# Two weight buffers for the modulation, eight tiles in the recurrence, and the channel DFT's fold computed early

## The chip, the cores and the metric

The kernel runs on one core of one Trainium2 chip. Its metric is the device time of one execution in microseconds (us). The time before is the median of three runs. The profile is of one further execution of its own.

## The reference, cut to what matters

The function is two layers of a diffusion backbone over 1024 latent tokens and 256 context tokens (1280 together), with a model width of 1024. Layer 0 is a bidirectional gated linear recurrence beside a Fourier mixer; layer 1 is latent attention. Each layer is modulated by a shift, a scale and a gate that come from a conditioning vector:

```python
def adaln(cond, w, b):
    return jnp.split(jax.nn.silu(cond) @ w + b, 3, axis=-1)      # w is 1024 x 3072, per layer

def rglru_coeffs(xc, gate_w, gate_b, lam):                       # per head of 64 channels, per direction
    r, i = sigmoid(gates of xc)
    log_a = -LRU_C * r * softplus(-lam)
    a = exp(log_a)
    b = sqrt(-expm1(2.0 * log_a)) * (i * xc)
    return a, b                                                  # then h[t] = a[t] * h[t-1] + b[t], both ways

def fourier_mix(u, w, b):
    ug = u.reshape(b_, length, FNET_GROUPS, FNET_GROUP_DIM)
    f = jnp.fft.fft2(ug, axes=(1, 3), norm='ortho').real
    return jnp.einsum('blgi,gij->blgj', f, w).reshape(b_, length, FNET_WIDTH) + b
```

In `fourier_mix` the transform over the 128 channels of a group and the 128 x 128 matrix `w` of that group are both linear maps of the channels, so the kernel folds them into one pair of tables: cos times `w` and sin times `w`.

## The kernel before

The kernel keeps the 1280 tokens in the free dimension and 128 channels in the partitions. Matrices of float32 are split into a high and a low part, and a product is three matmuls (high by high, high by low, low by high).

**Start (L145 to L308).** `ada_part` multiplies the condition with layer 0's shift and scale weights in four parts, from 32 loads of 256 KB through eight buffers (L209). `u0` (L238) loads one of eight tiles of the input through three buffers of the pool `xt`, modulates it and splits it into `uh` and `ul`. The word list `ORD` (L39) sets the order of these loads. The matmuls of the first two input projections, `in0(12)` and `in0(0)`, run as soon as their `uh` and `ul` are there.

**Recurrence (L445 to L521).** An input projection `in0(m)` (L262) is 24 groups of three matmuls (512, 512 and 256 tokens) into a PSUM tile `z`, of which there are two (L137). For each j from 0 to 6 the kernel runs `in0(j + 1)` and `in0(13 + j)`, that is 48 groups or slots, and hangs all other work of the recurrence on these slots through `slots0(j)` (L470). I call one such round of 48 slots a round. Among that work are six pieces of `gates` (L362), the convolution, the chain of tanh, exp, square, root and the two scans on ScalarE, VectorE and GpSimd (L383), the splits of the next weights (`w0_high` on VectorE, `w0_low` on GpSimd) and `ada_next` (L461).

**The modulation's other weights.** Layer 1's shift and scale (`adam`, L173) and both layers' gates (`adag`) are 16 units in `ada_work` (L252): each loads 1 MB (L174), multiplies it by the condition in eight matmuls (L165) into a tile of the PSUM pool `g_ps`, which has two tiles (L138) and also serves the gates, and adds the result to a row on VectorE (L183). Two further entries without a load finish a row. A round calls `ada_next` at slots 0, 38 and 44 while units are left, which is in rounds 0 to 5. The pool `adaw` (L312) has one buffer of 1 MB, so the load for a unit can start only when the matmuls of the unit before it are done, and `ada_next` issues it right behind them.

**Order.** Inside `manual_schedule` (L459) the order on TensorE, VectorE, ScalarE and GpSimd is the one that `slots0` writes down. The order of the loads on SyncE (SP) is left to the framework's scheduler, which issues a load when it takes its buffer to be free; on the chip SP then waits, in order, for each load's buffer.

**Tiles of the recurrence.** `lt` (L359) hands out tiles of 128 x 1280 from a ring of nine: per round r and i of both directions, th and aa of both directions, eight in all.

**Fourier mixer (L534 on).** The pool `ft` is opened when the recurrence's pools are closed, so its tiles lie where tiles of the recurrence were, and a load or a write into it waits for the last use of what lay there. The folded tables `cw` and `sw` (L134) are computed here: `fw`, `cosd` and `sind` are loaded from ScalarE's queue (L541 to L544), and in `fourier(0)` (L561) two float32 matmuls of 512 columns, `dft_c` and `dft_s`, write two `g_ps` tiles which ScalarE copies to `cw` and `sw`. Before them in TensorE's order stands `in0(9)`; behind them stand the first transform matmuls `aps` (L605), which read `cw`, and `in0(10)`, which needs the PSUM tile that `in0(8)` has filled and that ScalarE's copy `fu` (L567) empties.

Of the kernel before, what the change touches and what calls it, by code (L numbers as in the profile page):

```python
# [13 lines left out]
F32 = mybir.dt.float32  # L14
# [7 lines left out]
P = 128  # L22
# [31 lines left out]
def _body(ctx, tc, ap, out, dbg=None):  # L54
# [42 lines left out]
    o = 0  # L97
# [31 lines left out]
    V.tensor_scalar(out=vneg, in0=vpos, scalar1=-8.0, scalar2=None, op0=ALU.mult)  # L129
    V.tensor_scalar(out=vpos, in0=vpos, scalar1=8.0, scalar2=None, op0=ALU.mult)  # L130
    sp_c()


    cw = const.tile([P, 512], F32, name="cw")  # L134
    sw = const.tile([P, 512], F32, name="sw")
# [173 lines left out]
            u0(i)  # L309
    xt_c()  # L310
    a0_c()
    aw_p, aw_c = pool("adaw", 1, side="right")  # L312

    lru = None

# [40 lines left out]
        else:  # L356
            V.tensor_tensor(out=hls[j][1], in0=xcs[j], in1=f(hls[j][0]), op=ALU.subtract)

    def lt(nm):  # L359
        return lru.tile([P, T], F32, tag="lt", bufs=9, name=nm)  # L360

    def gates(j, d, c):  # L362

        def run():
            a, n = CH3[c]
            if c == 0:
                for g in range(2):
                    gt[j, d, g] = lt(f"gate{d}{g}_{j}")
            gh, gl = gws[j]
            xh, xl = hls[j]  # L370
            ps = [gtile(f"gps{j}{d}{c}{h}") for h in range(2)]
            for i, (w, x) in enumerate(((gh, xh), (gh, xl), (gl, xh))):
                for h in range(2):
                    r = slice(64 * h, 64 * h + 64)
                    TE.matmul(ps[h][:, :n], w[r, d, :], x[r, a : a + n], start=(i == 0), stop=(i == 2))  # L375
            for h in range(2):
                for g in range(2):
                    r = slice(64 * g, 64 * g + 64)
                    S.activation(out=gt[j, d, g][64 * h : 64 * h + 64, a : a + n], in_=ps[h][r, :n], func=AF.Sigmoid,  # L379
                                 bias=vv("gateb", 4 * j + 2 * h + d)[r, :])  # L380
        return run

    def chain(j):  # L383

        c = {}

        def tanh(d):
            th[j, d] = lt(f"th{d}_{j}")
            S.activation(out=th[j, d], in_=gt[j, d, 0], func=AF.Tanh, scale=vpos[:, 8 * d + j : 8 * d + j + 1])

        def exp(d):
            aa[j, d] = lt(f"aa{d}_{j}")
            S.activation(out=aa[j, d], in_=gt[j, d, 0], func=AF.Exp, scale=vneg[:, 8 * d + j : 8 * d + j + 1])

        def square(d):
            S.activation(out=gt[j, d, 0], in_=aa[j, d], func=AF.Square)

        def beta(d):
            V.scalar_tensor_tensor(out=th[j, d], in0=gt[j, d, 0], scalar=1.0, in1=th[j, d], op0=ALU.add, op1=ALU.mult)  # L399

        def root(d):
            S.activation(out=th[j, d], in_=th[j, d], func=AF.Sqrt)

        def drive(d):
            G.tensor_tensor(out=gt[j, d, 1], in0=gt[j, d, 1], in1=xcs[j], op=ALU.mult)

        def scaled(d):
            V.tensor_tensor(out=gt[j, d, 1], in0=gt[j, d, 1], in1=th[j, d], op=ALU.mult)  # L408

        def scan(d):  # L410
            r, i, a = th[j, d], gt[j, d, 1], aa[j, d]
            if d == 0:
                c1, c2, e = slice(0, NC), slice(NC, T), slice(NC - 1, NC)
            else:
                c1, c2, e = slice(NC - 1, None, -1), slice(T - 1, NC - 1, -1), slice(0, 1)
            V.tensor_tensor_scan(out=r[:, c1], data0=a[:, c1], data1=i[:, c1], initial=0.0, op0=ALU.mult, op1=ALU.add)  # L416
            V.tensor_tensor_scan(out=r[:, c2], data0=a[:, c2], data1=i[:, c2], initial=r[:, e], op0=ALU.mult, op1=ALU.add)

        def both():
            G.tensor_tensor(out=th[j, 0], in0=th[j, 0], in1=th[j, 1], op=ALU.add)  # L420
            if "hs" in dbg:
                load(dbg["hs"][j], th[j, 0])

        def gated():
            sg = sgs_.pop(j)
            V.tensor_tensor(out=sg, in0=sg, in1=th[j, 0], op=ALU.mult)
            put(j, sg)

        for n, u in (("tanh", tanh), ("exp", exp), ("square", square), ("beta", beta), ("root", root),
                     ("drive", drive), ("scaled", scaled), ("scan", scan)):  # L430
            for d in range(2):
                c[n, d] = lambda u=u, d=d: u(d)
        c["both"], c["gated"] = both, gated
        return c
# [19 lines left out]
    x_split(0, 1)  # L454
    w0_load(1)
    w0_dma(13)
    ada_work[0][0]()
    order0 = ExitStack()
    order0.enter_context(tc.manual_schedule(engines={e.engine for e in (TE, V, S, G)}))  # L459

    def ada_next():  # L461
        if ada_work:
            _, u = ada_work.pop(0)
            u()
        if ada_work and ada_work[0][0]:
            ada_work[0][0]()

    ch = {}

# [67 lines left out]
    evs = ft_p.tile([P, 640], F32, name="ev")  # L537
    ods = ft_p.tile([P, 640], F32, name="od")
    fold = ft_p.tile([P, 4, 256], F32, name="fold")
    fw = ft_p.tile([P, 512], F32, name="fw")  # L540
    S.dma_start(out=fw, in_=ap["fw"])  # L541
    dft = [ft_p.tile([P, P], F32, name=n) for n in ("cosd", "sind")]
    for d, n in zip(dft, ("cosd", "sind")):
        S.dma_start(out=d, in_=ap[n])  # L544
    tabs = {}
    for n in ("cos_h", "cos_l", "sin_h", "sin_l"):
        t = ft_p.tile([P, 2, 2, 256], F32R, name=n)
# [10 lines left out]
    def fourier(g, work=()):  # L558

        z = in0(8 + g, work) if g else z8  # L560
        if g == 0:  # L561
            for d, o, n in zip(dft, (cw, sw), "cs"):
                ps = gtile(f"dft_{n}")
                TE.matmul(ps, d, fw, start=True, stop=True)
                S.copy(out=o, in_=ps)
        u, ev, od = fus[g % 2], evs, ods
        S.copy(out=u, in_=z[:, :T])  # L567
        cg, sgm = cw[:, P * g : P * g + P], sw[:, P * g : P * g + P]
# [939 lines left out]
```

## Time and profile before

| | us |
|---|---|
| median of three runs | 1500.9 |
| the three runs | 1502.68, 1500.90, 1496.44 |
| the profiled execution | 1506.19 |
| its span in the profile | 1504.4 |

| engine | busy us | share of the span |
|---|---|---|
| TensorE matmul (PE) | 1416.8 | 94% |
| VectorE (DVE) | 944.1 | 63% |
| GpSimd (POOL) | 684.0 | 45% |
| ScalarE (ACT) | 597.2 | 40% |

The span is the time from the first to the last instruction of the profiled execution; the 1.8 us around it are not in the profile. The shares are means over stages with different limits, so the start (to about 63 us), the recurrence (63 to 392 us) and the entry of the Fourier mixer (392 to 430 us) have to be read for themselves. In a timeline row the text in square brackets is the time for which the engine stood idle before the row, and what ended it.

### The profile page before, as it was taken

The numbers are of one execution on the slowest core, as the hardware profiler recorded it, in microseconds if no ns is written. First come the engines' busy times: TensorE is split into PE (matmuls) and PEld (weight loads), VectorE is DVE, ScalarE is ACT, GpSimd is POOL, SyncE is SP. The second block draws the span as 40 slices with busy tenths as digits, with TensorE's granted clock in tenths as the row PEclk, the third lists the DMA queues.
The fourth block names the chain that finished last, engine by engine and source line by source line (L and its number), as shares of the span: only waits on it lengthen the run. The fifth ranks groups of instructions, "written<-read, shape, count | busy, mean of one in ns | idle before, by whom it ended". The sixth has DMA issues, their size and how long they took to land.

```text
span 1504.4 us, 19960 instructions
## 1 busy us (share of the span) xinstructions
PE 1416.8 (94%) x7912; PEld 993.6 (66%) x7912; DVE 944.1 (63%) x1454; ACT 597.2 (40%) x756; POOL 684.0 (45%) x314
## 2 busy tenths in 40 slices
PE   6978998898789999999999999999999999999996
PEld 3756675576568878887987675555555555555685
DVE  4538787799456524233954537576665757574799
ACT  2268676688611222111432133433443334445210
POOL 1124243344311114330422128766856776699642
PEclk9999999999989999999999999999999999999998
DMA  8522223311130455322043121101201010124442
GB/s 299 209 88 103 90 105 116 123 60 46 46 93 29 146 195 180 112 90 68 5 126 116 64 84 32 50 15 53 74 19 36 29 36 15 36 64 140 133 129 82
DMA packets 65869, 133.05 MB, mean 88 GB/s; under 512 B 5864, under 2 KB 32744, under 8 KB 63472
## 3 DMA queue, kind: packets, MB, share of 16 engines
q1 hardware_dynamic: 63328, 123.79, 25.3%
q0 software_dynamic: 2016, 7.60, 1.4%
q8 instruction: 62, 1.02, 0.3%
q10 hardware_dynamic: 432, 0.39, 0.1%
q14 instruction: 31, 0.25, 0.1%
HBM read 100.09 MB, written 24.66 MB: 83 GB/s over the span
## 4 chain that ended last, share of the span: by engine, by line
PE 62%; DVE 17%; issue 5%; DMA 4%; POOL 2%; ACT 1%; SPq 0%; DVEq 0%; POOLq 0%; ACTq 0%
PE s L1197 12%; PE y L770 10%; PE po L1213 10%; PE mx L1100 6%; PE z L270 5%; PE in1g L84 2%; PE in1g L86 2%; PE in1g L85 2%; DVE xc L339 2%; DVE hf L1384 1%; DMA adawg<-in_ada_g 1%; DVE gate L408 1%; DVE th L416 1%; POOL th L420 1%; DVE th L399 1%
## 5 line engine op out<-in xcount | busy, mean ns | idle before, releaser
L1203 POOL TENSOR_TENSOR ra<-ra,p 128x1024 f32<-128x1024 f32 x112 | 268.5, 2397 | 97.1 <-ACT p L1199 94.4
L1102 DVE TENSOR_REDUCE m<-mx 128x1 f32<-128x512 f32 (+1 forms) x384 | 210.1, 589 | 101.5 <-PE mx L1100 100.9
L1199 ACT ACTIVATE p<-s 128x1024 f32<-128x1024 f32 x160 | 163.3, 1024 | 210.5 <-PE s L1197 207.7
L293 POOL TENSOR_TENSOR w0l<-w,w0h 128x1024 fp32r<-128x1024 f32 x24 | 69.2, 2883 | 280.5 <-DVE w0h L77 196.4
L270 PE MATMUL z<-uh,w0h 128*128 128x512 f32 (+1 forms) x576 | 154.7, 376 | 4.4 <-ACT uh L75 4.3
L270 PE MATMUL z<-ul,w0h 128*128 128x512 f32 (+1 forms) x576 | 151.2, 370 | 0.0
L270 PE MATMUL z<-uh,w0l 128*128 128x512 f32 (+1 forms) x576 | 147.8, 364 | 0.0
L379 ACT ACTIVATE gate<-gps,vec 64x512 f32<-64x512 f32 (+1 forms) x192 | 117.4, 612 | 47.1 <-PE gps L375 44.2
L270 PEld LDWEIGHTS z<-uh,w0h 128*128 128x128 f32 x576 | 97.9, 194 | 39.4 <-issue 18.4
L270 PEld LDWEIGHTS z<-ul,w0h 128*128 128x128 f32 x576 | 97.8, 193 | 27.5 <-issue 10.0
L270 PEld LDWEIGHTS z<-uh,w0l 128*128 128x128 f32 x576 | 96.5, 191 | 21.2 <-issue 4.1
L1197 PE MATMUL s<-R,KR 33*128 33x512 f32 (+1 forms) x640 | 101.8, 392 | 0.0
L1100 PE MATMUL mx<-Kh,Qh 64*128 64x512 f32 (+1 forms) x384 | 84.1, 404 | 3.9 <-DVE m L1102 3.9
L1100 PEld LDWEIGHTS mx<-Kh,Qh 64*128 64x128 f32 x384 | 39.5, 185 | 70.6 <-DVE m L1102 31.9
L1213 PE MATMUL po<-p,v_odd 128*64 128x512 f32 x320 | 79.2, 616 | 0.0
L1213 PE MATMUL po<-p,v_even 128*64 128x512 f32 x320 | 79.1, 616 | 0.0
L1100 PE MATMUL mx<-KR,R 64*128 64x512 f32 (+1 forms) x384 | 73.0, 356 | 0.0
L1197 PE MATMUL s<-Qh,Kh 64*128 64x512 f32 x320 | 70.3, 431 | 0.0
L1197 PEld LDWEIGHTS s<-R,KR 33*128 33x128 f32 (+1 forms) x640 | 61.6, 184 | 12.9
L773 DVE TENSOR_TENSOR n<-gbc,y 128x1024 f32<-128x1024 f32 x10 | 12.2, 1221 | 85.9 <-PE y L770 85.9
L1238 DVE RECIPROCAL ri<-ri 128x128 f32<-128x128 f32 x64 | 59.3, 937 | 9.9 <-ACT ri L1233 9.9
L1197 PE MATMUL s<-Ql,Kh 64*128 64x512 f32 x320 | 64.0, 391 | 0.0
(358 smaller groups left out, 3021.5 us busy)
## 6 DMA issues: line engine op xcount, KB each, us to landing
w<-in_w SPq DMA_DIRECT2D x24, 512.0 KB
adaw<-in_ada SPq DMA_DIRECT2D x32, 256.0 KB
adawm<-in_ada SPq DMA_DIRECT2D x8, 1024.0 KB
adawg<-in_ada_g SPq DMA_DIRECT2D x8, 1024.0 KB
y_dr<-sg SPq DMA_DIRECT2D x10, 640.0 KB
woraw<-in_wo SPq DMA_DIRECT2D x12, 512.0 KB
xt<-in_x_cm SPq DMA_DIRECT2D x8, 640.0 KB
yra<-y_dr SPq DMA_DIRECT2D x10, 512.0 KB
```

The source lines that it names most:

```text
L84: TE.matmul(o, lh, rh, start=start, stop=False)
L270: TE.matmul(z[:, a : a + n], wi[:, kt, :], ui[kt][:, a : a + n], start=(kt == 0 and ui is uh and wi is wh), stop=(kt == KT - 1 and wi is wl))
L293: G.tensor_tensor(out=wl, in0=wr.pop(m), in1=f(wh), op=ALU.subtract)
L379: S.activation(out=gt[j, d, g][64 * h : 64 * h + 64, a : a + n], in_=ps[h][r, :n], func=AF.Sigmoid, bias=vv("gateb", 4 * j + 2 * h + d)[r, :])
L770: TE.matmul(ps[:, 512 * hf : 512 * hf + 512], a[k], b[k][:, 512 * hf : 512 * hf + 512], start=(k == 0 and a is yh and b is woh), stop=(k = ...
L1100: TE.matmul(ps[a][:, :n], q[r, P * t : P * t + P], k[r, a0 : a0 + n], start=st, stop=not st)
L1102: V.tensor_reduce(out=m3s[t][:, a, i : i + 1], in_=ps[a][:, :n], axis=AX.X, op=ALU.max)
L1197: TE.matmul(ps[:, a, :], k[r, ks], w[r, c], start=(j == 0), stop=(j == len(parts) - 1))
L1199: S.activation(out=es, in_=ps, func=AF.Exp, scale=SCALE)
L1203: G.tensor_tensor(out=ra, in0=st["e"][0] if kt == 1 else ra, in1=es, op=ALU.add)
L1213: TE.matmul(st["o"][64 * a : 64 * a + 64, :], quad[q][6][:, k, 128 * i + 64 * a : 128 * i + 64 * a + 64], st["e"][k][:, a, :], start=(k == ...
L1238: V.reciprocal(out=st["ri"][:, d], in_=st["ri"][:, d])
```

## The change

- The pool `adaw` gets two buffers. Two of its loads are issued ahead of the recurrence, and `ada_next` then issues the load of the unit after the next one.
- `lt` no longer takes the next of nine tiles. Eight tiles have fixed names, and a table says for each round which tile of the round before each new tile takes over.
- `fw`, `cosd` and `sind` are loaded, and `cw` and `sw` computed, between the start's pools and the recurrence, in a pool `dq` that is closed at once. The loads are now on SP's queue. The same lines go from the Fourier mixer.

```diff
@@ -309,7 +308,19 @@
             u0(i)
     xt_c()
     a0_c()
-    aw_p, aw_c = pool("adaw", 1, side="right")
+    aw_p, aw_c = pool("adaw", 2, side="right")
+
+
+    dq_p, dq_c = pool("dq", side="right")
+    fw = dq_p.tile([P, 512], F32, name="fw")
+    load(fw, ap["fw"])
+    for o, n, nm in ((cw, "cosd", "c"), (sw, "sind", "s")):
+        d = dq_p.tile([P, P], F32, name=n)
+        load(d, ap[n])
+        ps = gtile(f"dft_{nm}")
+        TE.matmul(ps, d, fw, start=True, stop=True)
+        S.copy(out=o, in_=ps)
+    dq_c()
 
     lru = None
 
@@ -356,8 +367,15 @@
         else:
             V.tensor_tensor(out=hls[j][1], in0=xcs[j], in1=f(hls[j][0]), op=ALU.subtract)
 
-    def lt(nm):
-        return lru.tile([P, T], F32, tag="lt", bufs=9, name=nm)
+
+    LT = ["r0", "i0", "r1", "i1", "th0", "th1", "aa0", "aa1"]
+    lts = {-1: {n: i for i, n in enumerate(LT)}}
+
+    def lt(j, n):
+        if j not in lts:
+            o = lts[j - 1]
+            lts[j] = dict(zip(LT, (o[k] for k in ("r0", "r1", "i0", "aa0", "i1", "aa1", "th0", "th1"))))
+        return lru.tile([P, T], F32, tag=f"lt{lts[j][n]}", name=f"{n}_{j}")
 
     def gates(j, d, c):
 
@@ -365,7 +383,7 @@
             a, n = CH3[c]
             if c == 0:
                 for g in range(2):
-                    gt[j, d, g] = lt(f"gate{d}{g}_{j}")
+                    gt[j, d, g] = lt(j, f"{'ri'[g]}{d}")
             gh, gl = gws[j]
             xh, xl = hls[j]
             ps = [gtile(f"gps{j}{d}{c}{h}") for h in range(2)]
@@ -385,11 +403,11 @@
         c = {}
 
         def tanh(d):
-            th[j, d] = lt(f"th{d}_{j}")
+            th[j, d] = lt(j, f"th{d}")
             S.activation(out=th[j, d], in_=gt[j, d, 0], func=AF.Tanh, scale=vpos[:, 8 * d + j : 8 * d + j + 1])
 
         def exp(d):
-            aa[j, d] = lt(f"aa{d}_{j}")
+            aa[j, d] = lt(j, f"aa{d}")
             S.activation(out=aa[j, d], in_=gt[j, d, 0], func=AF.Exp, scale=vneg[:, 8 * d + j : 8 * d + j + 1])
 
         def square(d):
@@ -454,7 +472,8 @@
     x_split(0, 1)
     w0_load(1)
     w0_dma(13)
-    ada_work[0][0]()
+    for k in range(2):
+        ada_work[k][0]()
     order0 = ExitStack()
     order0.enter_context(tc.manual_schedule(engines={e.engine for e in (TE, V, S, G)}))
 
@@ -462,8 +481,8 @@
         if ada_work:
             _, u = ada_work.pop(0)
             u()
-        if ada_work and ada_work[0][0]:
-            ada_work[0][0]()
+            if len(ada_work) > 1 and ada_work[1][0]:
+                ada_work[1][0]()
 
     ch = {}
 
@@ -537,11 +556,6 @@
     evs = ft_p.tile([P, 640], F32, name="ev")
     ods = ft_p.tile([P, 640], F32, name="od")
     fold = ft_p.tile([P, 4, 256], F32, name="fold")
-    fw = ft_p.tile([P, 512], F32, name="fw")
-    S.dma_start(out=fw, in_=ap["fw"])
-    dft = [ft_p.tile([P, P], F32, name=n) for n in ("cosd", "sind")]
-    for d, n in zip(dft, ("cosd", "sind")):
-        S.dma_start(out=d, in_=ap[n])
     tabs = {}
     for n in ("cos_h", "cos_l", "sin_h", "sin_l"):
         t = ft_p.tile([P, 2, 2, 256], F32R, name=n)
@@ -558,11 +572,6 @@
     def fourier(g, work=()):
 
         z = in0(8 + g, work) if g else z8
-        if g == 0:
-            for d, o, n in zip(dft, (cw, sw), "cs"):
-                ps = gtile(f"dft_{n}")
-                TE.matmul(ps, d, fw, start=True, stop=True)
-                S.copy(out=o, in_=ps)
         u, ev, od = fus[g % 2], evs, ods
         S.copy(out=u, in_=z[:, :T])
         cg, sgm = cw[:, P * g : P * g + P], sw[:, P * g : P * g + P]
```

## Rows read from the trace of the kernel before

**Rows 1.** The page, part 2: busy tenths of TensorE in 40 slices of the span.

```profile
PE   6978998898789999999999999999999999999996
```

**Rows 2.** Waits of TensorE, 0 to 430 us: waiter, released by, us, times, longest.

```profile
PE adam L165 <- DMA adawm<-in_ada: 11.9, 4, 5.4
PE adag L165 <- DMA adawg<-in_ada_g: 11.8, 4, 4.4
PE dft_c L564 <- DMA cosd<-in_cosd: 11.8, 1, 11.8
```

**Rows 3.** Timeline of TensorE, units at slots 0, 38, 44: start, us, what, [idle].

```profile
63.10 1.07 PE L165 MATMUL adam<-adawm,cond 128*32 128x512 f32 x8
...
105.00 1.94 PE L165 MATMUL adam<-adawm,cond 128*32 128x512 f32 x8 [5.39 <-DMA adawm<-in_ada]
...
111.82 1.07 PE L165 MATMUL adam<-adawm,cond 128*32 128x512 f32 x8 [1.34 <-DMA adawm<-in_ada]
...
141.39 1.06 PE L165 MATMUL adam<-adawm,cond 128*32 128x512 f32 x8
...
150.80 1.94 PE L165 MATMUL adam<-adawm,cond 128*32 128x512 f32 x8 [4.64 <-DMA adawm<-in_ada]
...
157.75 1.06 PE L165 MATMUL adam<-adawm,cond 128*32 128x512 f32 x8 [0.55 <-DMA adawm<-in_ada]
...
237.84 1.93 PE L165 MATMUL adag<-adawg,cond 128*32 128x512 f32 x8 [4.44 <-DMA adawg<-in_ada_g]
...
244.85 1.07 PE L165 MATMUL adag<-adawg,cond 128*32 128x512 f32 x8 [1.41 <-DMA adawg<-in_ada_g]
...
283.31 1.93 PE L165 MATMUL adag<-adawg,cond 128*32 128x512 f32 x8 [4.12 <-DMA adawg<-in_ada_g]
...
290.28 1.07 PE L165 MATMUL adag<-adawg,cond 128*32 128x512 f32 x8 [1.85 <-DMA adawg<-in_ada_g]
```

**Rows 4.** Windows: PE, PEld, DVE, ACT, POOL busy (count), PEclk, DMA share, GB/s.

```profile
150.80:155.50 4.70, 4.70 (x16) 2.56 (x17) 0.69 (x1) 0.28 (x1) 0.00 (x0) 0.50 0.32 90
290.28:326.21 35.93, 35.93 (x194) 26.80 (x194) 32.90 (x22) 27.89 (x35) 15.98 (x5) 1.00 0.23 78
```

**Rows 5.** Timeline of SP's queue, loads issued, 47 to 145 us.

```profile
47.62 1.19 SPq L60 DMA_DIRECT2D w<-in_w  x2
...
143.84 0.33 SPq L60 DMA_DIRECT2D w<-in_w  x1
144.26 0.38 SPq L60 DMA_DIRECT2D adawm<-in_ada  x1
```

**Rows 6.** Timeline of VectorE and ScalarE in round 1, 147 to 150 us.

```profile
148.01 0.67 DVE L183 TENSOR_TENSOR adarow<-adarow,adam 128x512 f32<-128x512 f32 x1
...
147.37 2.41 ACT L396 ACTIVATE gate<-aa 128x1280 f32<-128x1280 f32 x2
```

**Rows 7.** The end of the start: VectorE's timeline, then two windows.

```profile
52.53 2.91 DVE L81 TENSOR_TENSOR ul<-xt,uh 128x1280 fp32r<-128x1280 f32 x2
...
54.00:58.00 4.00, 4.00 (x23) 3.38 (x22) 2.13 (x3) 0.17 (x1) 0.00 (x0) 1.00 0.70 281
58.00:62.00 4.00, 4.00 (x22) 3.42 (x21) 1.69 (x2) 1.07 (x1) 3.15 (x2) 1.00 0.13 30
```

**Rows 8.** Timeline of TensorE and ScalarE at the Fourier mixer's entry, 416 to 426 us.

```profile
416.18 2.04 PE L564 MATMUL dft_c<-fw,cosd 128*128 128x512 f32 x2 [11.76 <-DMA cosd<-in_cosd]
418.01 1.89 PE L564 MATMUL dft_s<-fw,sind 128*128 128x512 f32 x2
424.32 2.04 PE L605 MATMUL aps0a<-cw,fold 128*128 128x128 f32 x8 [4.42 <-DVE fold L582]
...
419.76 2.35 ACT L567 COPY fu<-z 128x1280 f32<-128x1280 f32 x2 [14.35 <-DVE sg L426]
```

**Rows 9.** Timeline of VectorE and ScalarE in round 2, scan and second direction's gates.

```profile
167.19 2.35 DVE L417 TENSOR_TENSOR_SCAN th<-aa,th,gate 128x1024 f32<-128x1024 f32 x1
...
176.55 2.80 ACT L379 ACTIVATE gate<-gps,vec 64x512 f32<-64x512 f32 x4 [0.97 <-PE gps L375]
```

## The prediction

> **What bounds the kernel now.** I read the page's slices first, then the waits of TensorE, and then the timelines at the places that those waits name. In the slices TensorE is busy nearly everywhere; the lower digits lie in the first third [rows 1]. So time is to be gained only where TensorE stands still there. The waits name three such places among the changed code: the `adam` units wait 11.9 us for their loads, the `adag` units 11.8 us, and `dft_c` 11.8 us for `cosd` [rows 2]. The rest is not touched by the change.
>
> The timeline shows which units wait. In rounds 0, 1, 3 and 4 the unit at slot 44 waits 5.39, 4.64, 4.44 and 4.12 us for a load that was issued only when the unit at slot 38 was done, and the unit at the next round's slot 0 waits again for 1.34, 0.55, 1.41 and 1.85 us [rows 3]. Behind the longer wait TensorE runs at the lower of its two clock levels, 1.2 GHz: the granted clock is 0.50 from 150.80 to 155.50 us [rows 4], and the eight matmuls of the unit take 1.94 us where they take 1.06 without a wait [rows 3]. Round 2 has its last entry without a load, and round 5 has units at slots 0 and 38 alone and then a bare addition, so neither has this pattern.
>
> **The change, part by part.**
>
> *Two buffers.* The load issued behind the slot-38 unit now feeds not the next unit but the one after it, at slot 0 of the next round. The slot-44 unit finds its data, since they were asked for behind the slot-0 unit some forty slots earlier. What is late next is the slot-0 unit. I leave its load where it is in SP's queue: in round 1 it stands behind a weight load that SP releases at 143.84 us, is issued at 144.26 [rows 5], and is there when the unit starts at 150.80 [rows 3]. So the new start of the slot-0 unit is the old start of the slot-44 unit, and each of the four rounds becomes shorter by the difference of two rows [rows 3]:
> 111.82 - 105.00 = 6.82; 157.75 - 150.80 = 6.95; 244.85 - 237.84 = 7.01; 290.28 - 283.31 = 6.97; together 27.75 us.
> This holds the clock's part too. It holds only if TensorE is ready by then. In round 1 it may start the slot-44 unit at 150.80 - 4.64 = 146.16, and that unit with its four groups took 157.75 - 0.55 - 150.80 = 6.40 us at the half clock, so about 3.2 at the full one: it is ready at 149.4 and waits 1.4 us. The same sum gives 2.2, 1.2 and 0.9 us in rounds 0, 3 and 4: nearly 6 us of waiting stay, where there were 23.7.
> Nor may another engine be later than the load. The unit needs a `g_ps` tile that VectorE's addition of the slot-38 unit frees, and that ends at 148.01 + 0.67 = 148.68; the squares that the next round's first step needs end at 147.37 + 2.41 = 149.78 [rows 6]. Both are before 150.80, by 2.1 and 1.0 us. Can VectorE keep the shorter round? Round 5, with two units and no long wait, took 35.93 us at a VectorE busy for 32.90 of them, with TensorE never idle [rows 4]; the four rounds come down from about 46 to 39 us, which is longer. The first two loads go out together at the end of the start; the unit that needs the first stands at 63.10 [rows 3], and the transfer engines are at 0.13 of their time from 58 to 62 us [rows 7], so 1 MB more there is taken as free; without that room the slot-0 unit of round 0 would wait some 3.6 us, 1 MB at 281 GB/s [rows 7].
> Bounds of this part: if nothing is left to wait for at slot 0, the rounds save 9.0 + 8.4 + 8.2 + 7.9 = 33.5 us; if each remaining wait drops the clock as the long one does (4.7 us at half speed, 2.35 lost), they save 27.75 - 9.4 = 18.4. Idle times of 1.34 to 1.85 us were followed by units of 1.07 us, at the full clock [rows 3]; so I take 27.75.
>
> *The channel DFT at the Fourier entry.* Here 11.76 us of waiting and 3.72 us of matmuls (416.18 to 419.90) go [rows 8], but the path does not run through them. ScalarE's copy `fu` starts at 419.76, behind VectorE's last product of the recurrence, and the first transform at 424.32, behind VectorE's fold of that copy [rows 8]. By the pools' sizes `fu` still lies over a tile which that product reads, so both stay. What opens is that `in0(10)` may start when the first of the two copies is done, about 420.9, and fill TensorE until 424.32. This is worth 3.4 us if the scheduler places it before the transforms, and 0 if not. I take 1.2, nearer to nothing, as work behind a long idle time starts at the half clock.
>
> *The channel DFT at the start.* The same two matmuls, 3.72 us behind an idle TensorE, take half, 1.86, at the full clock, and they now lie where TensorE is busy for 4.00 of 4.00 us at a granted 1.00 [rows 7]: +1.86, between 0 and 3.72. `fw` lies in `dq` over the third buffer of `xt` (counting the pools from the right end of SBUF), whose last reader is the split `ul`, done at 52.53 + 2.91 = 55.44 [rows 7]. If the scheduler puts `dft_c` into TensorE's order before `fw` is there, `in0` queues behind it, and VectorE and GpSimd with the next weights behind that. Ahead of `fw` SP has 3.4 MB to load from about 47.6 us on [rows 5] (two weight tiles, two units, gate weights and a bias); at 281 GB/s [rows 7] that is done at 59.7, and 0.4 MB more at 61.0. So the wait is 0 to 61.0 - 55.4 = 5.6 us; I take 1.3, nearer to 0, because a place in the order later by some groups hides it. ScalarE gets two copies where it is busy for 1.07 of 4.00 us [rows 7], and its queue loses three loads; both count nothing.
>
> *A rule weighed.* These loads leave a queue of their own for SP's. The Trainium skill, "DMA: Bandwidth & Descriptors", section "Queues, rings and completion order", says that an engine takes the descriptors of one ring in order and alternates between different queues. By that rule the constants would have shared the engines from ScalarE's queue, and on SP's they come after all 3.4 MB: the wait would be 5.6 and not 1.3, and the sum 4.3 us higher. No row here shows two queues loading at once.
>
> *Eight tiles.* The gates of the second direction now write tiles that the first scan of the round before read last. That scan ends at 167.19 + 2.35 = 169.54 and the gates write from 176.55 [rows 9], a margin of 7.0 us counted within one round, which the change leaves alone; the first direction's gates stand in ScalarE's order behind the root that already waits for the last reader of their tiles. So 0.
>
> **The sum.** -27.75 + 1.86 + 1.3 - 1.2 = -25.8 us. The span of 1504.4 becomes 1478.6, the execution of 1506.2 becomes 1480.4. The median of the three runs is 5.3 us below the profiled one, so I set the sum against it: 1500.9 - 25.8 = 1475.
>
> **The rivals.**
> 1. *No wait is left*: the slot-0 load comes before 149 us because the scheduler moves it ahead of the weight load. Then the rounds save 33.5 and the time is 1469. For it: only SP's order holds the load back. Against it: that order has no reason to change.
> 2. *The constants come late*, behind all that SP has to load, or the remaining waits drop the clock: 5.6 us for `fw` gives 1479.4, the clock's 9.4 on top 1489. For it: SP's 3.4 MB. Against it: idle times under 2 us kept the clock.
> 3. *The second buffer doesn't help*: SP issues the load behind the slot-44 unit after all, the rounds keep their length and only the sum's rest stays, +2.0: 1503, within the bound of no change. Against it: in round 1 SP issued the load 1.8 us after the slot-38 unit's end.
> 4. *Slower, by the eight tiles*: if the first scan ends later than 18.8 us after the round's start (11.8 now), ScalarE's gates wait for it, hold both `g_ps` tiles, and TensorE stops, in seven rounds. It outweighs 25.8 us from 3.7 us a round, that is with the scan 10.7 us later than now; at 12 us later it costs 35 and gives 1510. Against it: VectorE starts each round afresh, waiting for the slot-0 unit.
>
> **How the numbers follow.** Forecast (1470 to 1482) 0.62; rival 1 (1463 to 1470) 0.15; rival 2 (1482 to 1493) 0.14; rival 3 (1493 to 1508) 0.05; rival 4 0.04. A measurement of this kernel can tell about 0.5%, 7.5 us, from no change, so faster holds the first three: 0.91, the same 0.05, slower 0.04. The range has to take in rival 1 with the open 3.4 us (1464) and most of rival 2: 1463 to 1490.
>
> **What the changed profile would show.** Right: the slot-44 units without an idle time, the slot-0 units with 1 to 2 us of it, the wait for `adam` and `adag` loads near 6 us in all, rounds 0, 1, 3 and 4 near 39 us, the granted clock at 1.00 through them, `fu` still behind the last product. Wrong: a wait of ScalarE's gates for VectorE's scan, a `dft_c` that stands idle for more than some 3 us at the start, or slot-0 units that wait for 5 us, which would show the load still behind the unit.

## The result: 1477 us, and the profile after

The changed kernel takes 1477.0 us (median of four runs, 1476.0 to 1477.7); the kernel before, beside it on the same chip, 1501.6. The ratio is 0.9842, with a 95% interval from 0.9819 to 0.9866: 24.6 us faster by the medians, where 25.8 were forecast, and inside the range. Its profiled execution took 1476.0 us at a span of 1474.3.

The page's slices first: TensorE's busy tenths and the granted clock in 40 slices of the changed kernel's span. The sevens and eights that stood in the third to the ninth slice in [rows 1] are nines now; the eleventh, with the Fourier entry, fell from 7 to 5.

```profile
PE   6999999998599999998999999999999999999997
...
PEclk9999999999799999999999999999999999999999
```

Then TensorE's waits of the changed kernel, 0 to 430 us (waiter, released by, us, times, longest). Against [rows 2] the units' waits have come down from 23.7 us in eight waits to 5.2 in four, and `dft_c` is gone from the list. A wait of 17.3 us behind ScalarE's copy `fu` stands in its place at the Fourier entry.

```profile
PE z L269 <- ACT fu L576: 17.3, 1, 17.3
...
PE adam L164 <- DMA adawm<-in_ada: 3.1, 2, 2.1
...
PE adag L164 <- DMA adawg<-in_ada_g: 2.1, 2, 1.4
```

The timeline of TensorE in the changed kernel: the first unit, the units at slots 44 and 0 around the ends of rounds 0, 1, 3 and 4, and at 188.17 the first unit of round 3 (start, us, what, idle time before). These answer to [rows 3].

```profile
65.84 1.07 PE L164 MATMUL adam<-adawm,cond 128*32 128x512 f32 x8
...
102.28 1.06 PE L164 MATMUL adam<-adawm,cond 128*32 128x512 f32 x8
107.96 1.07 PE L164 MATMUL adam<-adawm,cond 128*32 128x512 f32 x8 [2.09 <-DMA adawm<-in_ada]
...
142.22 1.06 PE L164 MATMUL adam<-adawm,cond 128*32 128x512 f32 x8
146.86 1.06 PE L164 MATMUL adam<-adawm,cond 128*32 128x512 f32 x8 [1.04 <-DMA adawm<-in_ada]
...
188.17 1.16 PE L164 MATMUL adag<-adawg,cond 128*32 128x512 f32 x8
...
222.55 1.07 PE L164 MATMUL adag<-adawg,cond 128*32 128x512 f32 x8
227.53 1.06 PE L164 MATMUL adag<-adawg,cond 128*32 128x512 f32 x8 [1.38 <-DMA adawg<-in_ada_g]
...
261.81 1.06 PE L164 MATMUL adag<-adawg,cond 128*32 128x512 f32 x8
266.15 1.07 PE L164 MATMUL adag<-adawg,cond 128*32 128x512 f32 x8 [0.74 <-DMA adawg<-in_ada_g]
```

No slot-44 unit waits any more, and each slot-0 unit waits 0.7 to 2.1 us. The clock that had gone to its lower level behind the long wait [rows 4] stays at 1.00 through round 1 (window of TensorE's busy time, granted clock in the third column from the end):

```profile
107.96:146.86 38.90, 37.85 (x205) 27.34 (x206) 34.58 (x24) 30.83 (x37) 17.05 (x6) 1.00 0.33 118
```

Where the time came from, at five points of the two profiled executions, before and after:

| point | before | after | so far | this stretch |
|---|---|---|---|---|
| first unit of round 0 | 63.10 | 65.84 | +2.74 | +2.74 |
| slot-0 unit of round 5 | 290.28 | 266.15 | -24.13 | -26.87 |
| `fu`, behind round 7 | 419.76 | 396.91 | -22.85 | +1.28 |
| first transform, `aps0a` | 424.32 | 401.47 | -22.85 | 0 |
| first `y` matmul of the Fourier branch | 536.56 | 510.31 | -26.25 | -3.40 |

From there to the end the two profiled spans differ by another 3.9 us. Nothing changed there, and the medians differ by 24.6 in all: the profiled execution of the kernel before lies 4.6 us above its median, the changed kernel's 1.0 below. In the twelve traces of this study that stretch, which no edit touches, takes from 957.8 to 967.8 us, and the kernel before has the longest. So I count the 3.9 us as a difference between two executions.

### The profile page after: what moved, and what is told of

Read it like the earlier page. It is cut to its first block, busy times and chain, and to the rows that moved or that the text cites. A ratio compares the mean times of both kernels' runs of the same rounds, so it can differ in the third digit from the quotient of the medians.

```text
span 1474.3 us, 19962 instructions
## 1 busy us (share of the span) xinstructions
PE 1405.3 (95%) x7912; PEld 988.1 (67%) x7912; DVE 943.4 (64%) x1454; ACT 603.1 (41%) x760; POOL 685.4 (46%) x314
## 3 DMA queue, kind: packets, MB, share of 16 engines
q1 hardware_dynamic: 63760, 124.18, 25.8%
## 4 chain that ended last, share of the span: by engine, by line
PE 60%; DVE 17%; issue 5%; DMA 4%; ACT 3%; POOL 3%; SPq 0%; DVEq 0%; POOLq 0%; ACTq 0%
PE s L1206 13%; PE y L779 10%; PE po L1222 10%; PE mx L1109 6%; PE z L269 3%; PE in1g L84 2%; PE in1g L86 2%; PE in1g L85 2%; DVE xc L350 2%; DVE th L417 2%; DVE hf L1393 1%; DVE th L434 1%; POOL th L438 1%; DVE i L426 1%; DVE th L435 1%
## 5 line engine op out<-in xcount | busy, mean ns | idle before, releaser
L269 PE MATMUL z<-uh,w0h 128*128 128x512 f32 (+1 forms) x576 | 152.1, 372 | 22.5 <-ACT fu L576 17.3
L1109 PEld LDWEIGHTS mx<-Kh,Qh 64*128 64x128 f32 x384 | 39.3, 185 | 69.6 <-DVE m L1111 33.3
L397 ACT ACTIVATE r<-gps,vec 64x512 f32<-64x512 f32 (+1 forms) x96 | 58.6, 610 | 45.3 <-PE gps L393 44.0
L782 DVE TENSOR_TENSOR n<-gbc,y 128x1024 f32<-128x1024 f32 x10 | 12.2, 1221 | 87.0 <-PE y L779 87.0
L423 POOL TENSOR_TENSOR i<-i,xc 128x1280 f32<-128x1280 f32 x16 | 57.1, 3572 | 18.5 <-ACT i L397 18.5
```

Source lines behind the costliest of these rows:

```text
L269: TE.matmul(z[:, a : a + n], wi[:, kt, :], ui[kt][:, a : a + n], start=(kt == 0 and ui is uh and wi is wh), stop=(kt == KT - 1 and wi is wl))
L1109: TE.matmul(ps[a][:, :n], q[r, P * t : P * t + P], k[r, a0 : a0 + n], start=st, stop=not st)
```

## The experiments

Each ratio below is against the kernel before on the same chip, with its 95% interval. To compare parts, one more sum is used: the lengths of rounds 0, 1, 3 and 4, each from its first slot-0 unit to the next, added up. It is 185.86 us before and 159.00 in the changed kernel.

### The changed kernel again

> The changed kernel itself, unaltered, beside the three others on one chip, so that they can be compared with it. Every theory: ratio to the kernel before 0.982 to 0.987, rounds 0 to 4 of 42.1, 38.9, 41.3, 39.4 and 38.6 us, 5.2 us of waiting for the units' loads.

Ratio 0.9835 [0.9811, 0.9859]; the four rounds sum to 158.94 us, and the units wait 3.9 us for loads. This is the repeat by which small differences are judged: single rounds agree within 0.3 us, but `fu` stood 1.0 us later behind round 7 than in the first trace.

The agreement hides a difference in round 1. Its first unit waited 1.93 us, and the clock fell behind it: the granted clock is 1.00 while the unit runs and 0.50 from 108.50 to 111.90 us, where the first trace has 1.00 behind a wait of 2.09 us.

```profile
107.53 1.06 PE L164 MATMUL adam<-adawm,cond 128*32 128x512 f32 x8 [1.93 <-DMA adawm<-in_ada]
108.52 1.44 PE L269 MATMUL z<-ul,w0h 128*128 128x512 f32 x3
```

The slot-38 unit of that round came 30.95 us behind the first unit, against 29.56 in the first trace. The round became only 0.28 us longer: the wait of 1.04 us before the next slot-0 unit is gone in its place.

### Two buffers and eight tiles, the DFT left in the mixer

```diff
...
-    fw = dq_p.tile([P, 512], F32, name="fw")
-    load(fw, ap["fw"])
...
+        if g == 0:
+            for d, o, n in zip(dft, (cw, sw), "cs"):
+                ps = gtile(f"dft_{n}")
+                TE.matmul(ps, d, fw, start=True, stop=True)
+                S.copy(out=o, in_=ps)
```

> The changed kernel with the channel DFT left in the Fourier mixer, so two buffers and eight tiles alone. Theory (the second buffer carries the gain): rounds 0, 1, 3 and 4 become shorter by the 26.9 us that the changed kernel's trace shows; round 0's first unit stays near the 63.1 us of before; the Fourier entry keeps dft_c's long wait and loses nothing of 132.3 us from aps0a to y. Sum near -25, time 1474 to 1478, the same as the changed kernel within 3 us. Rival (the early DFT carries a good part, since 11.8 us of waiting at dft_c went): 1485 to 1490.

Ratio 0.9836 [0.9816, 0.9856], 1474.0 us: all of the changed kernel's gain without the DFT's move. The four rounds sum to 158.15 us. From `aps0a` to `y` it takes 112.05 us, and 112.24 before (the expectation's 132.3 is not the length of this stretch). Two rows of TensorE at the start, and two at the Fourier entry:

```profile
49.77 0.33 PE L225 MATMUL adatr<-ident,adarow 128*128 128x128 f32 x1 [1.00 <-DVE adarow L223]
64.05 1.06 PE L164 MATMUL adam<-adawm,cond 128*32 128x512 f32 x8
...
393.01 2.04 PE L572 MATMUL dft_c<-fw,cosd 128*128 128x512 f32 x2 [14.55 <-DMA cosd<-in_cosd]
399.03 1.20 PE L613 MATMUL aps0a<-cw,fold 128*128 128x128 f32 x4 [2.27 <-DVE fold L590]
```

From the last transpose of the start, `adatr`, to the first unit are 64.05 - 49.77 = 14.28 us; before it was the same 14.28 (from 48.82, in the row below, to 63.10 [rows 3]). So the second buffer's first load costs nothing there. And `dft_c` waits 14.55 us for `cosd` without hurting: `aps0a` still waits for VectorE's fold after it.

```profile
48.82 0.33 PE L226 MATMUL adatr<-ident,adarow 128*128 128x128 f32 x1 [1.00 <-DVE adarow L224]
```

### The early DFT alone

```diff
     aw_p, aw_c = pool("adaw", 1, side="right")
+    dq_p, dq_c = pool("dq", side="right")
...
-            for d, o, n in zip(dft, (cw, sw), "cs"):
```

> The kernel before with the channel DFT moved beside the first projections and nothing else; one buffer, nine tiles. Theory (the path at the Fourier entry runs through ScalarE's copy fu, not through dft_c): +2.7 us at the first unit as in the changed kernel, -3.7 us from aps0a to y, rounds as before with the slot-44 units waiting 4 to 5 us; time 1498 to 1502. Rival (dft_c's wait of 11.8 us was on the path): 1488 to 1491.

Ratio 0.9974 [0.9954, 0.9995], a median 1.9 us below the kernel before: near the theory, and far from the 11.8 us of the rival. TensorE at the start, and its wait at the Fourier entry:

```profile
48.55 0.33 PE L226 MATMUL adatr<-ident,adarow 128*128 128x128 f32 x1 [1.00 <-DVE adarow L224]
...
53.27 1.02 PE L321 MATMUL dft_c<-fw,cosd 128*128 128x512 f32 x2
...
64.55 1.07 PE L165 MATMUL adam<-adawm,cond 128*32 128x512 f32 x8
```

```profile
PE z L270 <- ACT fu L569: 15.1, 1, 15.1
```

`adatr` to the first unit takes 16.00 us: the two matmuls cost 16.00 - 14.28 = 1.72 us, with no wait for `fw`. At the entry TensorE stands idle for 15.1 us all the same, now behind `fu`: the wait changed its name and stayed. (In this build `fu` lies over other tiles and waits for GpSimd's sum of the two scans, one step before the last product.) From `aps0a` (421.20) to the first `y` (530.41) it is 109.21 us, against 112.24 before and 112.05 with the DFT in the mixer.

### Eight tiles alone

```diff
-    def lt(nm):
-        return lru.tile([P, T], F32, tag="lt", bufs=9, name=nm)
...
+    def lt(j, n):
+        if j not in lts:
+            o = lts[j - 1]
+            lts[j] = dict(zip(LT, (o[k] for k in ("r0", "r1", "i0", "aa0", "i1", "aa1", "th0", "th1"))))
+        return lru.tile([P, T], F32, tag=f"lt{lts[j][n]}", name=f"{n}_{j}")
...
```

> The kernel before with eight named tiles in the order of release instead of the ring of nine, nothing else. Theory: the rounds keep their lengths to 0.3 us each (48.7, 45.9, 41.3, 45.8, 45.4), no wait of the gates for a scan; the tail behind round 7 becomes some 1.3 us longer, since ScalarE's order there now has direction 0's exponential, square and root between the gates of direction 1, with four more table loads; time 1500 to 1504. Rival (the gates wait for the first scan): +35, 1535. Rival (the order of release frees ScalarE earlier and gives a part of the changed kernel's gain): rounds shorter by 1 us or more each, below 1493.

Ratio 0.9992 [0.9977, 1.0006]: no difference. No gate waits for a scan; the four rounds sum to 184.69 us. Single rounds moved more than I had said (49.36, 46.09, 44.75 and 44.49 us), with the loads' waits, both ways; rounds 3 and 4 are the shorter ones, and there the slot-44 units took 1.06 and 1.10 us behind waits of 4.28 and 3.95, where they had taken 1.93 [rows 3]. The reordered tail is there, but its price can't be read here: in this build `fu` waits for the second scan and not for the last product; I take it that it lies over other tiles.

### Eight tiles, each kept for the same use

```diff
-            lts[j] = dict(zip(LT, (o[k] for k in ("r0", "r1", "i0", "aa0", "i1", "aa1", "th0", "th1"))))
+            lts[j] = o
```

> The changed kernel with its eight tiles each given to the same use in every round, in place of the order of release; every engine's order of instructions stays. Theory (the order of release is what hides the eighth tile): in the changed kernel's round 1 ScalarE writes the first i tile at 117.03 us, while the first scan, now that tile's last reader, ends at 119.77; so the gates wait 2.7 us in each of rounds 1 to 7, hold both g_ps tiles, and TensorE waits 1 to 2.7 us a round: +7 to +19 us, forecast 1490. Rival (ScalarE's idle times of 0.9 us between gates and the free g_ps tile take it up): gates wait for VectorE, TensorE doesn't, +0 to +3, 1477 to 1480.

Ratio 0.9963 [0.9949, 0.9978], 1494.8 us: 18 us slower than the changed kernel, at the upper end of the theory's bounds. Waits of ScalarE, then of TensorE, from the first round to the last:

```profile
ACT i L397 <- DVE th L435: 15.2, 6, 2.8
```

```profile
PE gps L393 <- ACT i L397: 14.0, 14, 1.6
```

In the changed kernel TensorE's line reads 1.5 us. The 12.5 us that came on top are not all: behind two such waits in round 3, of 1.47 and 0.91 us, the clock falls to its lower level. A window of this kernel shows it, with the granted clock third from the end:

```profile
210.00:215.00 5.00, 5.00 (x15) 4.02 (x15) 3.25 (x3) 2.54 (x4) 2.93 (x1) 0.50 0.02 3
```

So an eighth tile at no cost rests on the order of release, and this run is the fourth rival's mechanism made to happen, at an earlier place: the gates that wait are the first direction's (in round 1 at 119.81 us, 11.9 behind its first unit), where the rival had named the second's.

### One buffer, units further apart

```diff
-        put_(38, ada_next)
-        put_(44, ada_next)
+        put_(26, ada_next)
+        put_(38, ada_next)
```

> The kernel before, one buffer and nine tiles, with the three units of a round at slots 0, 26 and 38 instead of 0, 38 and 44. Theory (a unit waits because only six slots, some 5 us, lie between the release of the one buffer and its next use): 10 to 26 slots cover the load, the slot-38 unit has no wait, the slot-0 unit 0 to 2 us; rounds 0, 1, 3 and 4 near 39 us, sum -24 to -31, time 1470 to 1477. Rival (one buffer can't be enough, since the release always comes behind the unit): the 4 to 5 us waits move to the new slots and the time stays 1497 to 1503. Rival (the unit at slot 26 takes a PSUM tile from the gates of slots 24 to 29 and stalls them): rounds between 41 and 45 us, time 1480 to 1495.

Ratio 0.9975 [0.9956, 0.9994], 1495.3 us: my theory fell. The four rounds sum to 178.10 us, where I had expected about 156. Two things stood in the way. First SP's order, in this kernel's round 3: the unit at slot 38, done at 226.21 us, frees the buffer (the expectation of the last run below calls it the unit at slot 26, which starts at 212.87), but its load goes behind `gw`, 4.6 us later. TensorE's units and SP's queue:

```profile
225.14 1.07 PE L165 MATMUL adag<-adawg,cond 128*32 128x512 f32 x8
236.01 1.07 PE L165 MATMUL adag<-adawg,cond 128*32 128x512 f32 x8 [3.75 <-DMA adawg<-in_ada_g]
```

```profile
230.41 0.33 SPq L60 DMA_DIRECT2D gw<-in_gw  x1
230.84 6.62 SPq L60 DMA_DIRECT2D adawg<-in_ada_g  x2
```

Second the third explanation: a unit among the gates holds one of the two `g_ps` tiles until VectorE adds it up, and the gates' matmuls wait 8.1 us for that in rounds 0 to 4.

```profile
PE gps L375 <- DVE adarow L183: 5.1, 3, 2.1
...
PE gps L375 <- DVE adarowg L183: 3.0, 2, 1.7
```

Of the 7.8 us that the four rounds save, only 3.7 arrive in the time. Round 5 has a unit among its gates too, waits 1.24 us for VectorE and runs at a mean granted clock of 0.92 (280.58 to 325 us), against 1.00 in [rows 4]; from its first unit to `fu` it takes 136.14 us, against 129.48.

### SP's loads in written order, in the changed kernel

```diff
-    order0.enter_context(tc.manual_schedule(engines={e.engine for e in (TE, V, S, G)}))
+    order0.enter_context(tc.manual_schedule(engines={e.engine for e in (TE, V, S, G, nc.sync)}))
```

> The changed kernel with SP's loads in the recurrence held in the order in which the program writes them, so that the units' loads go ahead of the next round's weights (w) and gate weights (gw); all other engines' orders stay. Theory (the remaining wait at slot 0 comes from SP's order alone: in round 1 w goes at 139.99 us and the load at 140.41, while its buffer was free at 138.6; in round 0 the load stands behind gw until 102.62 while its buffer was free at 98.7): the slot-0 units lose the 2.1, 1.0, 1.4 and 0.7 us of waiting, -5 us, 1471 to 1473. Rival (the load's own time from the release of the buffer sets it): the waits stay within 1 us in all, 1476 to 1478. Rival (the weights, now behind, come late, or w behind y_dr's store): new waits at z for w0h, 1480 or more.

Ratio 0.9785 [0.976, 0.981], 1469.6 us: 7.2 us below the changed kernel beside it. The units of round 1 on TensorE and the load on SP:

```profile
136.13 1.06 PE L164 MATMUL adam<-adawm,cond 128*32 128x512 f32 x8
140.84 1.07 PE L164 MATMUL adam<-adawm,cond 128*32 128x512 f32 x8
144.36 1.07 PE L164 MATMUL adam<-adawm,cond 128*32 128x512 f32 x8
```

```profile
137.26 5.03 SPq L60 DMA_DIRECT2D adawm<-in_ada  x2
```

The load goes 0.07 us behind the unit that frees its buffer (137.19) and no unit waits. The four rounds sum to 153.44 us, 5.6 less than in the changed kernel.

### The same, and ScalarE's order behind round 7

```diff
     c = ch[7]
+    tail = ExitStack()
+    tail.enter_context(tc.manual_schedule(engines={S.engine}))
...
     c["gated"]()
+    tail.close()
```

> As the run with SP's loads in written order, and besides ScalarE's order behind round 7 held as the program writes it (no exponential, square or root between the gates of direction 1, four table loads less). Theory (that order, which came with the eight tiles, cost the changed kernel 1.25 us from round 7's first gate to fu): 1 to 1.5 us less than that run, 1470 to 1472. Rival (fu is set by VectorE's and GpSimd's part of the tail): the same as that run.

Ratio 0.9773 [0.9746, 0.98], 1465.9 us: the fastest kernel of this study, though its interval overlaps that of the run above. From the last round's sigmoid of the gate branch to `fu`, on ScalarE, with the third piece of that round's gates between them, first with SP's order alone and then with both:

```profile
342.54 1.24 ACT L457 ACTIVATE sg<-z 128x1280 f32<-128x1280 f32 x1
...
353.76 0.47 ACT L397 ACTIVATE r<-gps,vec 64x256 f32<-64x256 f32 x1 [3.21 <-PE gps L393]
...
393.07 2.35 ACT L576 COPY fu<-z 128x1280 f32<-128x1280 f32 x2 [9.29 <-DVE sg L444]
```

```profile
342.71 1.24 ACT L457 ACTIVATE sg<-z 128x1280 f32<-128x1280 f32 x1
...
353.41 0.47 ACT L397 ACTIVATE r<-gps,vec 64x256 f32<-64x256 f32 x1 [2.69 <-PE gps L393]
...
392.00 2.35 ACT L579 COPY fu<-z 128x1280 f32<-128x1280 f32 x2 [14.71 <-DVE sg L444]
```

50.53 and 49.29 us: 1.24 less, as expected. But the changed kernel's two traces have 49.57 and 50.55 for the same stretch. What differs between them is ScalarE's wait for TensorE before the third piece, 2.26 and 3.23 us. Counted from that piece on, the stretch takes 39.31 us here with SP's order alone, 38.59 with both, and 39.30 and 39.31 in the changed kernel's traces: the order is worth 0.7 us, and the rest of the 1.24 is that wait.

### SP's loads in written order, in the kernel before

The same line as two sections above, in the kernel before.

> The kernel before, one buffer, units at slots 0, 38 and 44, with only SP's loads of the recurrence held in written order; the other engines' orders stay. Theory (one buffer can't serve units six and four slots apart, whatever SP's order): the slot-44 unit's load goes at once behind the slot-38 unit (1.8 us earlier in round 1), so its wait falls from 4 to 5.4 us to about 3; the slot-0 unit's load still starts only behind the slot-44 unit and its wait grows, to some 2 or 3 us. Waits 15 to 22 us in all of 23.7, rounds 43 to 46 us, time 1490 to 1498. Rival (SP's order was the cause of the waits, the second buffer only one way round it): rounds of 38 to 40 us, 1470 to 1478.

Ratio 0.9897 [0.9872, 0.9922], 1486.7 us: between the two theories and nearer to mine, which had the slot-44 wait at about 3 us, since it didn't count that a load alone on the queue also lands sooner. The units' waits for loads come to 12.2 us in six, below the 15 to 22 that I had expected. Round 1 on TensorE, and SP's load:

```profile
137.06 1.07 PE L165 MATMUL adam<-adawm,cond 128*32 128x512 f32 x8
143.06 1.07 PE L165 MATMUL adam<-adawm,cond 128*32 128x512 f32 x8 [1.23 <-DMA adawm<-in_ada]
149.12 1.06 PE L165 MATMUL adam<-adawm,cond 128*32 128x512 f32 x8 [2.46 <-DMA adawm<-in_ada]
```

```profile
138.19 12.37 SPq L60 DMA_DIRECT2D adawm<-in_ada  x3
```

The four rounds sum to 170.13 us, 15.7 less than before, with one buffer still. From the end of one unit to the start of the next there are now 143.06 - 138.13 = 4.93 and 149.12 - 144.13 = 4.99 us: this is the load's own time here, from the release of the buffer to the next use, and one buffer of 1 MB doesn't go below it in any row of this run.

### One buffer, units apart, SP in written order

Both edits of the two runs with one buffer.

> The run with units at slots 0, 26 and 38 and one buffer, now with SP's loads of the recurrence in written order; the other engines' orders stay. Theory (what kept that run slow was first SP's order: in its round 3 the unit at slot 26 was done at 226.2 us and the next load went at 230.84, behind gw): no wait for adam and adag loads (11.7 us before), the 8 to 9 us in which gates' matmuls wait for VectorE's adarow stay; rounds 0, 1, 3 and 4 of 40 to 42 us, time 1480 to 1485. Rival (one buffer is too few even for units 10 slots apart): the loads' waits stay above 6 us, 1490 to 1496.

Ratio 0.9909 [0.9888, 0.993], 1488.4 us. TensorE's waits in the recurrence:

```profile
PE gps L375 <- DVE adarow L183: 5.6, 3, 2.1
PE gps L375 <- DVE adarowg L183: 5.2, 3, 1.7
...
PE adam L165 <- DMA adawm<-in_ada: 0.5, 1, 0.5
```

The loads' waits fell from 11.7 to 0.5 us, so SP's order was their cause and one buffer is enough for units that far apart. The gates' wait for VectorE stayed, 10.8 us in rounds 0 to 5 (9.3 before SP's order was held), and the sum of the four rounds is 167.27. Rounds 1, 3 and 4 are in the theory's bounds, round 0 (44.19 us) is 2.2 us above them and the time 3.4. From round 5's first unit to `fu`, outside that sum, it takes 133.59 us, against 129.48 before.

## Why the prediction was right

**The rounds: right in place and size.** Forecast -27.75 us, by round -6.82, -6.95, -7.01 and -6.97; measured -6.60, -7.03, -6.42 and -6.81, together -26.86. The waits that were to stay at slot 0, 2.2, 1.4, 1.2 and 0.9 us, came out at 2.09, 1.04, 1.38 and 0.74. That these fit so well is in part luck: the 3.2 us that I had taken for a unit and its four groups at the full clock are 3.6 in all four rounds (107.96 - 2.09 - 102.28 = 3.59), but counted from the slot-38 unit the loads too were there up to 0.5 us later than before. The step that carried this, that SP's order stays as it is and so the slot-0 load comes when the slot-44 load came, held: in the changed kernel's round 1 the weights go at 139.99 us and the load behind them.

```profile
139.99 0.33 SPq L60 DMA_DIRECT2D w<-in_w  x1
140.41 0.38 SPq L60 DMA_DIRECT2D adawm<-in_ada  x1
```

The runs show what the old wait was made of, which the prediction only carried along as a whole. In round 1 the slot-38 unit and the slot-44 unit stood 9.41 us apart before [rows 3], and 6.00 with SP in written order. Of the 3.41 us, 1.74 lie before the issue: 144.26 - 141.39 = 2.87 us from the unit's start to the load, against 138.19 - 137.06 = 1.13. The other 1.67 lie behind it: 6.54 us from issue to unit against 4.87, where a weight load of 0.5 MB had gone 0.42 us earlier. In round 0 only 0.13 MB of gate weights had gone ahead (at 99.51 us, the load at 99.93), and it took 5.07 us; so I put the 1.67 down to the weights. The Trainium skill, "DMA: Bandwidth & Descriptors", section "Queues, rings and completion order", says that descriptors of one ring are taken in order; these rows agree. Half the clock then cost the unit itself 1.94 - 1.07 = 0.87 us.

So there were two causes, and they overlap. The sum of the four rounds, in us:

| | SP's order as scheduled | SP in written order |
|---|---|---|
| one buffer | 185.86 | 170.13 |
| two buffers | 159.00 | 153.44 |

The kernels with two buffers also have the eight tiles and the early DFT; by themselves the tiles left 184.69 of the 185.86, and two buffers without the early DFT have 158.15, so neither makes the table's larger steps.

The second buffer is worth 26.9 us by itself and 16.7 behind the other; the order 15.7 and 5.6. The first rival's 33.5 us of rounds without any wait were 32.4 when a run made it happen, by the means that it named. The second buffer also hides most of the fault in SP's order, which is why the prediction could be right without naming it as a cause.

**The DFT at the start: right in sum, not in its parts.** Forecast +3.16 (1.86 for the matmuls, 1.3 for a wait for `fw`); measured +2.74, and +2.87 counted from `adatr`. The matmuls cost 1.72, by the early DFT alone. The wait for `fw` doesn't exist; instead VectorE's product `sg` came late, since ScalarE copies `cw` and `sw` ahead of its sigmoid, and TensorE waits 0.88 us for it. I had counted those copies at nothing. The last 0.3 us of the 2.87 have no wait that shows. TensorE at the start of the changed kernel, and its load of `fw`:

```profile
59.84 1.02 PE L321 MATMUL dft_c<-fw,cosd 128*128 128x512 f32 x2
...
65.06 0.85 PE L269 MATMUL z<-uh,w0h 128*128 128x512 f32 x3 [0.88 <-DVE sg L459]
```

```profile
55.37 0.33 SPq L60 DMA_DIRECT2D fw<-in_fw  x1
```

The rule that I weighed cost nothing here. I had put 3.4 MB ahead of `fw` on SP; it was issued as soon as the split that held its buffer ended (55.35 us), ahead of the second unit's load and the gate weights, with two weight tiles and one unit (2 MB) before it, and `dft_c` starts 4.5 us behind its issue without a wait.

**The Fourier entry: the path was right, the value too small.** Forecast -1.2 with a bound of -3.4; measured -3.40. The 11.76 us of waiting for `cosd` were worth nothing, as said, and `fu` still waits for the last product. What I put in the middle, whether `in0(10)` is ordered ahead of the first transform, turned out at the bound: it fills TensorE from 398.19 to 401.47 us.

```profile
398.19 1.44 PE L269 MATMUL z<-uh,w0h 128*128 128x512 f32 x3 [17.28 <-ACT fu L576]
...
401.47 2.05 PE L614 MATMUL aps0a<-cw,fold 128*128 128x128 f32 x8
```

Together the DFT's move brings 0.5 to 0.7 us in the traces (-3.40 against +2.74 or +2.87), and in the times nothing that shows: 0.9836 without it, 0.9835 with it.

**Eight tiles: 0, as forecast.** The margin of 7 us held: in the changed kernel's round 2 the first scan ends at 158.66 us and the second direction's gates write from 165.58. Without the order of release the same eight tiles cost 18 us, so the fourth rival had its mechanism right; the gates that then waited were the first direction's, and in the change itself it lacked a cause.

**Not foreseen.** The new tiles let the scheduler interleave ScalarE's last round differently, with four more table loads, and `fu` came 1.2 us later behind round 7 in the traces. Counted from the third piece of that round's gates to `fu`, in all traces where `fu` waits for the last product, it takes 38.5 to 38.6 us with the old order (five kernels) and 39.3 with the new one (four traces of three kernels). So the order costs 0.7 to 0.8 us. The rest lies before that piece, where ScalarE waits for TensorE, 1.82 us before and 2.26 after; over the traces with either order that wait goes from 1.8 to 3.2 us.

**The sum: close, in part by luck.** The parts of the two traces add up to -26.25 us at the first `y`, where -25.8 were forecast, but the errors offset: the rounds gave 0.9 us less, the start cost 0.4 less, the Fourier entry gave 2.2 more, and the last rounds lost 1.3 that I had not foreseen.

## What to carry to other kernels

When a matmul waits for a load, read two rows of the loading queue before adding a buffer: when the buffer came free, and when the load was issued. If something else stands between them, order is part of the cause and costs one line to mend; if not, the load's own time against the distance to the next use says whether a second buffer is needed. And a long wait on the list is only worth what lies behind it on the path: `dft_c`'s 11.8 us of idle time came back under another name.

## What the runs showed of the hardware

The length of an idle time alone didn't say whether TensorE's clock fell to its lower level behind it. The units' eight matmuls take 1.06 us at 2.4 GHz and 1.94 at 1.2. In the run with units apart a wait of 2.27 us in round 1 was followed by 1.94; in the run of eight tiles alone waits of 4.28 and 3.95 us were followed by 1.06 and 1.10. The changed kernel shows both behind the first unit of round 1: a granted clock of 1.00 behind a wait of 2.09 us in one trace, and of 0.50, from just behind the unit on, after one of 1.93 us in the other. In the run with each tile kept in its place, waits of 1.47 and 0.91 us came before the fall. So the prediction's assumption that idle times under 2 us keep the clock, read from four rows, is not a rule of this kernel; it held for every unit of the first trace, and in the second its failure cost round 1 0.28 us, since the lost time came out of the wait before that round's end.
